# A hybrid transformer layer in one launch: the joints of its two MLP products, and which engine multiplies in its closing norm

## The chip, the cores and the metric

The kernel runs on one core of a Trainium2 chip. The metric is the device time of one launch, in microseconds. The core's engines are called as in the profile: PE is TensorE (matmuls), PEld its weight load, DVE is VectorE, ACT ScalarE, POOL GpSimd, and SP (SyncE) issues the DMAs of the queue that matters here. Each engine works through its own list of instructions in order; semaphores make one wait for another.

## What is computed

One layer on 2048 tokens of width 1024, in fp32: a modulated input projection feeds attention heads and RWKV heads, an output projection joins them, and a norm and an MLP close the layer. The change concerns the last two lines of this, the end of the first norm and the whole MLP (hidden width 4096):

```python
def layer_norm(x, gain, bias):
    return (_normalize(x, LN_EPS) * gain + bias).astype(x.dtype)
def squared_relu_mlp(h, w1, w2):
    return jnp.square(jax.nn.relu(h @ w1)) @ w2
...
x = layer_norm(ALPHA * x + g1 * y, ln1_g, ln1_b)
x = layer_norm(ALPHA * x + g2 * squared_relu_mlp(modulate(x, sh2, sc2), mlp_w1, mlp_w2), ln2_g, ln2_b)
```

## The kernel before

A scheduler (the tile framework) takes the instructions in program order and sets from it, from the buffers and from the data each needs, the order in which each engine gets them. Loads and stores of these stages stand in SyncE's queue in the order in which they are issued. A named tile has a number of buffers (bufs); a new use of it waits until the oldest user is done.

**Seven products.** Both MLP products are done as 2x2 blocks by a scheme with seven block products in place of eight. The products are worked in the order MORD = (1, 5, 6, 3, 7, 2, 4). Operands are sums and differences of blocks. Each operand is held as two parts: a high part, cast to the format that TensorE takes (fp32r) by ScalarE, and a low part, the operand less its high part, made by VectorE. Each block pair then takes three matmuls: high by high, high by low, low by high.

**First product, mlp1.** The weights come in 32 groups, 16 for each half of the tokens; a group is one 128x8x256 tile (1.05 MB) in one of two buffers. Per group seven products of 12 matmuls each (L1513). prep(n) makes the weight operand of product n, three products ahead of the matmuls (M1LEAD): a sum on VectorE where there is one (w1s, L1438 to L1447), the cast w1h on ScalarE (L1452), the low part w1l on VectorE (L1453). When product 4 of group g is prepared, its buffer is done with, and the weights of group g+2 are loaded. The token operands are made once for each half: those of products 1, 5 and 6 before mlp1 starts (xstep), and those of 3, 7, 2 and 4 are written to DRAM (XU), read back by xload, and split by xsplit into xh (ScalarE, L1465) and xl (VectorE, L1466). The norm of the last two token tiles (xlast, norm1, L1351 to L1360) is done within groups 0 and 1; in it GpSimd multiplies by the gain (L1355), and VectorE adds the bias (L1356). Groups 4 to 11 also make the token operands for the second half. Results go through ReLU and square, are combined, and are stored to DRAM (HU, L1525).

**Second product, mlp2.** For each token half, four groups of hidden rows, each with seven products of one or two units. A unit is 24 matmuls (L1699) and takes a pair of hidden rows' tiles (al, 128x2x512, 0.52 MB, loaded from HU by hload, L1605) and weights (wp, 1.05 MB, wload, L1600). ScalarE casts ah and uh (L1654, L1610), VectorE makes the low parts (L1655, L1610). Ahead of the first hidden tile stand the four weight loads of the first group and two of the next. PSUM results are copied or added into acc (L1706, L1708).

**Closing, mlp_end.** At the end of each half what is left of the hidden rows (two of the sixteen blocks) is done as plain products (192 matmuls, L1782), with operands from std_prep (L1739). Eight rows of 128x1024 are finished one after the other: multiply by g2 (L1765, on VectorE for the rows in VMUL, otherwise on GpSimd), add ALPHA times the residual (L1766, VectorE), add the plain products from PSUM (L1784, VectorE, frees the buffers psqa and psqb), mean and variance (ScalarE, with small VectorE steps, L1795, L1799, L1800), multiply by the gain l2g (L1803, VectorE from row LGV on, otherwise GpSimd), add the bias l2b (L1804, VectorE), store. The last two rows of the second half are normalized on VectorE alone (L1787 to L1790). While half 0 is closed, the operands of half 1 are already being made.

## Time and profile before

| | us |
|---|---|
| three runs | 3502.34, 3503.34, 3514.05 |
| median | 3503.34 |
| profiled execution | 3507.75 |
| its span | 3506.0 |

The granted clock of TensorE, over the profiled span, is 0.954 of full speed. The first product's matmuls begin at 2180 us of the span, the second's at 2851.8, its second token half at about 3169, and the last matmul ends at 3485.5. The change touches nothing ahead of the output projection, whose end is at about 2160. Times in a timeline count from the span's start. "Idle before" is how long the engine stood still ahead of an instruction, and the name behind the arrow is what came last before it could start.

### The profile page before, as it was taken

The numbers are of one execution on the slowest core, as the hardware profiler recorded it, in microseconds if no ns is written. First come the engines' busy times: TensorE is split into PE (matmuls) and PEld (weight loads), VectorE is DVE, ScalarE is ACT, GpSimd is POOL, SyncE is SP. The second block draws the span as 40 slices with busy tenths as digits, with TensorE's granted clock in tenths as the row PEclk, the third lists the DMA queues.
The fourth block names the chain that finished last, engine by engine and source line by source line (L and its number), as shares of the span: only waits on it lengthen the run. The fifth ranks groups of instructions, "written<-read, shape, count | busy, mean of one in ns | idle before, by whom it ended". The sixth has DMA issues, their size and how long they took to land. (4 is left out here: it accounts for less than half of the span.)

```text
span 3506.0 us, 65269 instructions
## 1 busy us (share of the span) xinstructions
PE 3204.8 (91%) x25176; PEld 2608.2 (74%) x25176; DVE 2606.6 (74%) x4891; ACT 1522.6 (43%) x2891; POOL 553.2 (16%) x551
## 2 busy tenths in 40 slices
PE   7999999899948988899979987999999979999997
PEld 3878898789746766677756765777788858887886
DVE  5568887979696668668568867766767657898888
ACT  4555565456524444444532223333433344336433
POOL 0000000000013454444433321000000000021004
PEclk9999999999978999999989988999999989999998
DMA  7487367636775464554354546566544455445441
GB/s 247 134 245 216 86 175 183 174 97 171 196 181 136 99 147 115 131 124 124 94 175 152 165 149 216 192 196 210 206 156 141 147 178 169 160 160 193 146 156 66
DMA packets 765338, 561.67 MB, mean 160 GB/s; under 512 B 380412, under 2 KB 653564, under 8 KB 763620
## 3 DMA queue, kind: packets, MB, share of 16 engines
q1 hardware_dynamic: 691738, 523.14, 51.0%
q10 hardware_dynamic: 73290, 34.37, 3.4%
q8 instruction: 198, 3.24, 0.4%
q14 instruction: 112, 0.92, 0.1%
HBM read 359.70 MB, written 197.66 MB: 159 GB/s over the span
## 5 line engine op out<-in xcount | busy, mean ns | idle before, releaser
L449 PE MATMUL psm<-xh,wh 128*128 128x386 f32 (+1 forms) x1104 | 380.5, 347 | 16.0 <-ACT row L452 10.2
L449 PE MATMUL psm<-xl,wh 128*128 128x386 f32 (+1 forms) x1104 | 380.8, 345 | 2.4 <-DVE xl L420 2.2
L449 PE MATMUL psm<-xh,wl 128*128 128x386 f32 (+1 forms) x1104 | 377.0, 341 | 0.0
L449 PEld LDWEIGHTS psm<-xh,wh 128*128 128x128 f32 x1104 | 210.2, 191 | 42.2 <-ACT row L452 19.3
L1513 PE MATMUL psa<-xh,w1h 128*128 128x512 f32 x512 | 203.8, 398 | 25.9 <-ACT w1h L1452 19.7
L1765 POOL TENSOR_TENSOR acc<-acc,g 128x1024 f32<-128x1024 f32 x12 | 42.2, 3541 | 1154.6 <-DVE acc L1708 1154.6
L449 PEld LDWEIGHTS psm<-xl,wh 128*128 128x128 f32 x1104 | 210.4, 191 | 17.4 <-issue 7.3
L449 PEld LDWEIGHTS psm<-xh,wl 128*128 128x128 f32 x1104 | 210.3, 190 | 5.0 <-issue 3.7
L1654 ACT CAST ah<-al 128x1024 fp32r<-128x1024 f32 x98 | 103.0, 1051 | 235.2 <-DMA al<-HU 226.0
L1513 PE MATMUL psa<-xl,w1h 128*128 128x512 f32 x512 | 202.1, 395 | 0.0
L1513 PE MATMUL psa<-xh,w1l 128*128 128x512 f32 x512 | 201.0, 393 | 0.3 <-DVE w1l L1453 0.3
L1655 DVE TENSOR_TENSOR al<-al,ah 128x1024 fp32r<-128x1024 f32 x98 | 120.7, 1231 | 100.1 <-ACT ah L1654 99.9
L1699 PE MATMUL psqa<-uh,ah 128*128 128x512 f32 x400 | 156.9, 395 | 29.3 <-ACT uh L1610 22.2
L759 DVE TENSOR_TENSOR stmp<-mp,xp 128x9 f32<-128x9 f32 (+30 forms) x310 | 167.4, 540 | 20.9 <-DMA mp<-LB 8.9
L435 DVE TENSOR_TENSOR wl<-wst,wh 128x1024 fp32r<-128x1024 f32 x81 | 98.8, 1219 | 93.4 <-ACT wh L434 74.1
L1452 ACT CAST w1h<-w1s 128x512 fp32r<-128x512 f32 x96 | 59.6, 621 | 232.1 <-DVE w1s L1441 84.9
L1133 PE MATMUL psg<-ks,bkc 64*64 64x128 f32 (+1 forms) x1152 | 98.4, 289 | 65.2 <-DMA ks<-AR 63.1
L1699 PE MATMUL psqa<-ul,ah 128*128 128x512 f32 x400 | 156.9, 392 | 0.0
L1699 PE MATMUL psqa<-uh,al 128*128 128x512 f32 x400 | 156.6, 392 | 0.0
L760 DVE TENSOR_REDUCE xp<-stmp 128x3 f32<-128x9 f32 (+30 forms) x310 | 153.9, 497 | 3.4
L1699 PE MATMUL psqb<-ul,ah 128*128 128x512 f32 x384 | 149.4, 389 | 0.0
L1699 PE MATMUL psqb<-uh,al 128*128 128x512 f32 x384 | 149.4, 389 | 0.0
(394 smaller groups left out, 8932.3 us busy)
## 6 DMA issues: line engine op xcount, KB each, us to landing
al<-HU SPq DMA_DIRECT2D x106, 512.0 KB, 3.7
wst<-in_w_in SPq DMA_DIRECT2D x81, 512.0 KB, 4.5
w<-in_mlp_w SPq DMA_DIRECT2D x32, 1024.0 KB, 7.9
wp<-in_mlp_w SPq DMA_DIRECT2D x32, 1024.0 KB, 6.1
wmod<-in_w_mod SPq DMA_DIRECT2D x48, 512.0 KB, 5.1
HU<-p SPq DMA_DIRECT2D x96, 256.0 KB, 4.4
HU<-s SPq DMA_DIRECT2D x84, 256.0 KB, 2.0
bkc<-BK SPq DMA_DIRECT2D x36, 512.0 KB, 3.7
```

Source lines behind the costliest of these rows:

```text
L435: nc.vector.tensor_tensor(wl, w, f32(wh), ALU.subtract)
L449: nc.tensor.matmul(ps[:, :y - x], lhsT=s[:, k, :], rhs=m[:, k, x:y], start=(i == 0), stop=(i == 23))
L759: nc.vector.tensor_tensor(tv, mp[:, i:i + 1, lo:lo + n].to_broadcast([128, n, n]), xp[:, lo:lo + n, lo:lo + n], ALU.mult)
L760: nc.vector.tensor_reduce(xp[:, lo:lo + n, i], tv, AX.X, ALU.add)
L1133: nc.tensor.matmul(ps[u, p, 0:w], lhsT=bk[o, d, p, u], rhs=ks[h][o, d, p, 0:w], start=True, stop=True)
L1452: nc.scalar.copy(h, x)
L1513: nc.tensor.matmul(ps, lhsT=w[:, k, :], rhs=x[:, k, :], start=(i == 0 and pr in (1, 5, 2)), stop=(i == 11), skip_group_check=True)
L1654: fs += [lambda: nc.scalar.copy(ah, f32(al)), fb[0], lambda: V.tensor_tensor(al, f32(al), f32(ah), ALU.subtract), fb[1]]
L1655: lambda: V.tensor_tensor(al, f32(al), f32(ah), ALU.subtract), fb[1]]
L1699: nc.tensor.matmul(ps, lhsT=x[:, c, s], rhs=y[:, c, :], start=(i == 0 and new), stop=(i == 5 and end), skip_group_check=True)
L1765: (V if 4 * i + j in VMUL else G).tensor_tensor(row, row, g2, ALU.mult)
```

## The change

1. VMUL grows from rows (0, 1) to (0, 1, 2, 3) and LGV is removed. So GpSimd does eight of the g2 multiplies in place of twelve, and none of the twelve gain multiplies; VectorE does them.
2. The first two groups of mlp1 are interleaved: products 1, 5, 6 of both groups, then 3, 7, 2, 4 of both. The splits of loaded token operands come one product later and are issued behind the weight operand of a named product (issue_after, as elsewhere in this kernel). w1s gets four buffers.
3. The norm of the last two token tiles moves from groups 0 and 1 to 2 and 3, with its gain and bias rows loaded at group 1; the transposes move to groups 5 to 12.
4. At group 20 of mlp1 the first weights of mlp2 and the two hidden tiles of its first two units are loaded, into buffers that are free by then (m2first). The rows l2g, l2b and g2 get buffers of their own and are loaded at unit 8. The hidden tiles rotate over four buffers of one pool and two of another, in place of six of one. HU and XU become two DRAM tensors each, one for each half.
5. The loop that overlaps the output projection with the first xsteps does two of them per tile.

```diff
--- before.py
+++ after.py
@@ -49,8 +49,7 @@
 
-LGV = (6, 6)
-VMUL = (0,1)
+VMUL = (0, 1, 2, 3)
 CLEAD = 2
 
 
@@ -93,8 +92,8 @@
-        self.HU = scr("HU", [2, 16, 128, 7, 512])
-        self.XU = scr("XU", [2, 128, 7, 4, 512])
+        self.HU = [scr("HU%d" % i, [16, 128, 7, 512]) for i in range(2)]
+        self.XU = [scr("XU%d" % i, [128, 7, 4, 512]) for i in range(2)]
@@ -875,12 +874,14 @@
                     self.xu[pr] = [self.xp.tile([128, 4, 512], F32R, name="x%s%d" % (v, pr)) for v in "hl"]
                 self.w1 = {}
                 self.w1load(0)
-                m = 0
-                for i, _ in enumerate(tiles):
-                    for m in range(m, min(m + 3, 8)):
+                todo = list(range(8))
+                more = True
+                while more:
+                    for m in todo[:2]:
                         self.xstep(0, m // 2, m % 2)
-                    m += m < 8
-                assert m == 8
+                    del todo[:2]
+                    more = next(tiles, 0) is None
+                assert not todo
         with ExitStack() as e1:
             self.mlp1(e1)
         ex.close()
...
@@ -1424,8 +1425,10 @@
-        seq = [(g, pr) for g in range(NG) for pr in MORD]
-        sums, units = {}, {}
+
+        seq = [(g, pr) for ps in (MORD[:3], MORD[3:]) for g in range(2) for pr in ps]
+        seq += [(g, pr) for g in range(2, NG) for pr in MORD]
+        sums, units, made = {}, {}, {}
 
         def prep(n):
             if n >= len(seq):
@@ -1434,7 +1437,7 @@
             if pr == 5:
-                x = sums[g] = sp.tile([128, 4, 128], F32, name="w1s", bufs=2)
+                x = sums[g] = sp.tile([128, 4, 128], F32, name="w1s", bufs=4)
                 V.tensor_tensor(x, a21, a22, ALU.add)
             elif pr == 6:
                 x = sums[g]
@@ -1449,21 +1452,22 @@
                 x = {1: a11, 2: a12, 4: a22}[pr]
             h = up.tile([128, 4, 128], F32R, tag="w1u", name="w1h", bufs=10)
             l = up.tile([128, 4, 128], F32R, tag="w1u", name="w1l", bufs=10)
-            nc.scalar.copy(h, x)
-            V.tensor_tensor(l, x, f32(h), ALU.subtract)
+            made[n] = nc.scalar.copy(h, x).ins, V.tensor_tensor(l, x, f32(h), ALU.subtract).ins
             units[n] = h, l
...
         def xload(q, pr):
-            nc.sync.dma_start(f32(self.xu[pr][1]), self.XU[q, :, XU[pr]])
-
-        def xsplit(pr, src=None):
+            nc.sync.dma_start(f32(self.xu[pr][1]), self.XU[q][:, XU[pr]])
+
+        def xsplit(pr, n, src=None):
             h, l = self.xu[pr]
             src = f32(l) if src is None else src
-            nc.scalar.copy(h, src)
-            V.tensor_tensor(l, src, f32(h), ALU.subtract)
+            with self.tc.issue_after(made[n][0]):
+                nc.scalar.copy(h, src)
+            with self.tc.issue_after(made[n][1]):
+                V.tensor_tensor(l, src, f32(h), ALU.subtract)
 
...
-        todo = {n + 1: [lambda pr=pr: xsplit(pr)] for n, pr in enumerate(MORD[3:])}
+
+        todo = {n + 2: [lambda pr=pr, n=n: xsplit(pr, n + 3)] for n, pr in enumerate(MORD[3:])}
...
             if pr == 1:
-                if g < 2:
-
-                    if g == 0:
-                        rows = self.base.tile([128, 2, 1024], F32, tag="uk", name="l1gb")
-                        for i, v in enumerate(("ln1_g", "ln1_b")):
-                            nc.sync.dma_start(rows[:, i], a[v].to_broadcast([128, D]))
+                if g == 1:
+                    rows = self.base.tile([128, 2, 1024], F32, tag="uk", name="l1gb")
+                    for i, v in enumerate(("ln1_g", "ln1_b")):
+                        nc.sync.dma_start(rows[:, i], a[v].to_broadcast([128, D]))
+                elif g in (2, 3):
+
                     self.flush()
                     x, xn = [self.base.tile([128, 1024], F32, tag="t4", name=v, bufs=2) for v in ("xlast", "xnlast")]
-                    r = OB[-1] + g * 128
+                    r = OB[-1] + (g - 2) * 128
                     nc.sync.dma_start(x, self.X1[r:r + 128, :])
                     self.norm1(x, slice(r, r + 128), xn, rows[:, 0], rows[:, 1], osm)
-                elif g == 2:
+                elif g == 4:
                     self.flush()
-                elif 4 <= g < 12:
-                    if g == 4:
+                elif 5 <= g < 13:
+                    if g == 5:
                         self.uk = self.base.tile([128, 8, 256], F32, tag="uk", name="uk")
-                    self.xstep(1, (g - 4) // 2, g % 2)
+                    self.xstep(1, (g - 5) // 2, (g - 5) % 2)
                 elif g == 14:
                     u1 = self.base.tile([128, 4, 512], F32, tag="uk", name="u1")
-                    nc.sync.dma_start(u1, self.XU[1, :, XU[1]])
+                    nc.sync.dma_start(u1, self.XU[1][:, XU[1]])
+                elif g == 20:
+
+                    w = self.base.tile([128, 2, 1024], F32, tag="uk", name="wp")
+                    nc.sync.dma_start(w, self.w2rows(0, 0))
+                    hs = [self.hload(self.base, "t4", 2, 0, 2 * i, 1) for i in range(2)]
+                    self.m2first = w, hs
...
-                    xsplit(1, u1)
+                    xsplit(1, n + 1, u1)
                 else:
                     xload(1, pr)
-                    todo.setdefault(n + 4, []).append(lambda pr=pr: xsplit(pr))
+                    todo.setdefault(n + 4, []).append(lambda pr=pr, n=n: xsplit(pr, n + 5))
...
+    def w2rows(self, fg, i):
+        return self.a["mlp_w2"].rearrange("(c i p) n -> i p c n", i=2, p=128)[i, :, fg:fg + 2, :]
+
+    def hload(self, pool, tag, bufs, half, fg, pr):
+        t = pool.tile([128, 2, 512], F32R, tag=tag, name="al", bufs=bufs)
+        self.nc.sync.dma_start(f32(t), self.HU[half][fg:fg + 2, :, XU[pr]].rearrange("c p t -> p c t"))
+        return t
 
 
 
@@ -1581,9 +1601,8 @@
-        nc.sync.dma_start(g2, self.G[1].to_broadcast([128, D]))
-        lg, lb = [self.base.tile([128, D], F32, tag="t4", name=x, bufs=2) for x in ("l2g", "l2b")]
-        cnt = [0]
+        lg, lb = [cp.tile([128, D], F32, name=x) for x in ("l2g", "l2b")]
+        cnt = [1, 2]
 
         def c8(name):
             cnt[0] += 1
@@ -1594,16 +1613,15 @@
         def u3(name):
             return up.tile([128, 2, 512], F32R, tag="u3", name=name, bufs=16)
 
-
         def wload(fg, i):
             t = c8("wp")
-            nc.sync.dma_start(t, a["mlp_w2"].rearrange("(c i p) n -> i p c n", i=2, p=128)[i, :, fg:fg + 2, :])
+            nc.sync.dma_start(t, self.w2rows(fg, i))
             return t
 
         def hload(half, fg, pr):
-            t = up.tile([128, 2, 512], F32R, tag="al", name="al", bufs=6)
-            nc.sync.dma_start(f32(t), self.HU[half, fg:fg + 2, :, XU[pr]].rearrange("c p t -> p c t"))
-            return t
+            cnt[1] += 1
+            pool, tag, bufs = (self.base, "t4", 2) if cnt[1] % 6 in (1, 2) else (up, "al", 4)
+            return self.hload(pool, tag, bufs, half, fg, pr)
 
         def split(x):
             h, l = u3("uh"), u3("ul")
@@ -1663,18 +1681,23 @@
                 f()
             del fs[:k]
 
-        for f in wloads(0, 0):
+        ws[0, 0, 0, 0], (hs[0], hs[1]) = self.m2first
+        first = wloads(0, 0)[1:]
+        for n in range(2, M2LEAD + ALEAD):
+            if first:
+                first.pop(0)()
+            aload(n, 0)
+        for f in first:
             f()
-        for n in range(M2LEAD + ALEAD):
-            aload(n, 0)
         for n in range(M2LEAD):
             for f in lead(n):
                 f()
-        for t, x in ((lg, "ln2_g"), (lb, "ln2_b")):
-            nc.sync.dma_start(t, a[x].to_broadcast([128, D]))
         for n, (half, g, pr, kk) in enumerate(seq):
             m = n + M2LEAD
             aload(m + ALEAD, half)
+            if n == 8:
+                for t, x in ((lg, a["ln2_g"]), (lb, a["ln2_b"]), (g2, self.G[1])):
+                    nc.sync.dma_start(t, x.to_broadcast([128, D]))
...
-                (V if r >= LGV[half] else G).tensor_tensor(row, row, lg, ALU.mult)
+                V.tensor_tensor(row, row, lg, ALU.mult)
                 V.tensor_tensor(row, row, lb, ALU.add)
             t = base[4 * i + j]
             nc.sync.dma_start(a["out"][t:t + 128, :], row)
```

ScalarE's list at the entry of mlp1, before; xh<-xl is the split of a loaded token operand, w1h the cast of a weight operand (w a loaded block, w1s a sum):

```order
L1385 CAST xh_24328<-uk 128x256
L1465 CAST xh_25079<-xl_25080 128x2048
L1452 CAST w1h<-w_24330 128x512
L1452 CAST w1h<-w1s 128x512
L1465 CAST xh_25081<-xl_25082 128x2048
L208 ACTIVATE ors<-omv,eps 128x1
L1452 CAST w1h<-w1s 128x512
L1465 CAST xh_25083<-xl_25084 128x2048
```

The same place after the change:

```order
L1386 CAST xh_24330<-uk 128x256
L1455 CAST w1h<-w_24332 128x512
L1455 CAST w1h<-w1s 128x512
L207 ACTIVATE ors<-omv,eps 128x1
L1455 CAST w1h<-w1s 128x512
L1455 CAST w1h<-w_25111 128x512
L1468 CAST xh_25081<-xl_25082 128x2048
L1455 CAST w1h<-w1s 128x512
```

The first weight casts stood behind a token operand's cast, and that one behind its load; now four weight casts stand ahead of it.

SyncE's queue between the products, before; HU<-p and HU<-z are the last stores of mlp1, g the row g2:

```order
L1525 DMA HU<-p_30089 128x512
L1584 DMA g_30199<-G_93 128x1024
L1600 DMA wp<-in_mlp_w 128x2x1024 x2
L1525 DMA HU<-z_30171 128x512
L1600 DMA wp<-in_mlp_w 128x2x1024 x4
L1605 DMA al<-HU 128x2x512 x12
L1600 DMA wp<-in_mlp_w 128x2x1024
```

The same place after the change (HU_90 and HU_91 are the two halves' tensors):

```order
L1536 DMA HU_91<-p_30097 128x512
L1618 DMA wp<-in_mlp_w 128x2x1024 x3
L1536 DMA HU_91<-z_30179 128x512
L1618 DMA wp<-in_mlp_w 128x2x1024 x3
L1700 DMA l2g<-in_ln_g 128x1024
L1700 DMA l2b<-in_ln_b 128x1024
L1700 DMA g_30207<-G_95 128x1024
L1590 DMA al<-HU_90 128x2x512 x10
L1618 DMA wp<-in_mlp_w 128x2x1024
```

The first load of hidden rows in this place stood behind one row and six weight loads; it is now the third unit's, and stands behind six weight loads and three rows.

VectorE's list between the halves, before; acc<-psqa and acc<-psqb are the additions that free the PSUM buffers:

```order
L1784 TENSOR_TENSOR acc<-psqa,acc 128x512
L1795 TENSOR_SCALAR zmu<-zmu 128x1
L1804 TENSOR_TENSOR acc<-acc,l2b 128x1024
L1799 RECIPROCAL zrs_32314<-zrs_32314 128x1
L1800 TENSOR_SCALAR znb<-zmu,zrs_32314 128x1
L1784 TENSOR_TENSOR acc<-psqb,acc 128x512
L1804 TENSOR_TENSOR acc<-acc,l2b 128x1024
L1799 RECIPROCAL zrs_32375<-zrs_32375 128x1
L1795 TENSOR_SCALAR zmu<-zmu 128x1
L1784 TENSOR_TENSOR acc<-psqa,acc 128x512
```

The same place after the change:

```order
L1807 TENSOR_TENSOR acc<-psqa,acc 128x512
L1827 TENSOR_TENSOR acc<-acc,l2b 128x1024
L1823 TENSOR_SCALAR znb<-zmu,zrs_32272 128x1
L1826 TENSOR_TENSOR acc<-acc,l2g 128x1024
L1818 TENSOR_SCALAR zmu<-zmu 128x1
L1822 RECIPROCAL zrs_32316<-zrs_32316 128x1
L1807 TENSOR_TENSOR acc<-psqb,acc 128x512
L1827 TENSOR_TENSOR acc<-acc,l2b 128x1024
L1823 TENSOR_SCALAR znb<-zmu,zrs_32316 128x1
L1826 TENSOR_TENSOR acc<-acc,l2g 128x1024
L1807 TENSOR_TENSOR acc<-psqa,acc 128x512
```

Between one psqa addition and the next stood two bias additions; now two bias additions and two gain multiplies stand there.

## Rows read from the trace of the kernel before

**Rows 1.** Busy table of the page: engine, busy us, share of the span, instructions.
```profile
PE 3204.8 (91%) x25176; PEld 2608.2 (74%) x25176; DVE 2606.6 (74%) x4891; ACT 1522.6 (43%) x2891; POOL 553.2 (16%) x551
```

**Rows 2.** TensorE's timeline, entry: start, us, instruction, partitions x elements, [idle before <-releaser].
```profile
2180.02 0.79 PE L1513 MATMUL psa<-xh,w1h 128*128 128x512 f32 x1 [19.38 <-ACT w1h L1452]
```

**Rows 3.** ScalarE's timeline, entry of the first product.
```profile
2177.55 1.90 ACT L1465 CAST xh<-xl 128x2048 fp32r<-128x2048 f32 x1 [12.96 <-DMA xl<-XU]
```

**Rows 4.** VectorE's timeline, entry of the first product.
```profile
2174.34 0.69 DVE L1438 TENSOR_TENSOR w1s<-w 128x512 f32<-128x512 f32 x1 [6.17 <-DMA w<-in_mlp_w]
...
2195.24 1.22 DVE L1356 TENSOR_TENSOR xlast<-xlast,l1gb 128x1024 f32<-128x1024 f32 x1 [2.27 <-POOL xlast L1355]
```

**Rows 5.** Windows: stretch, us, engines' busy time; then one of L1513 alone (PE, PEld).
```profile
2174.30:2236.50 62.20, 50.93 (x199) 38.74 (x200) 53.66 (x79) 26.16 (x41) 8.41 (x2) 0.90 0.59 217
...
2228.45:2248.75 20.30, 19.39 (x85) 15.57 (x84) 1.00 0.72 232
```

**Rows 6.** GpSimd's timeline, entry of the first product.
```profile
2189.18 6.02 POOL L1355 TENSOR_TENSOR xlast<-xlast,l1gb 128x1024 f32<-128x1024 f32 x1 [38.36 <-DMA l1gb<-in_ln_b]
```

**Rows 7.** ScalarE's timeline, between the products.
```profile
2830.29 0.63 ACT L1560 ACTIVATE z<-z 128x512 f32<-128x512 f32 x1
...
2849.79 1.04 ACT L1654 CAST ah<-al 128x1024 fp32r<-128x1024 f32 x1 [18.87 <-DMA al<-HU]
```

**Rows 8.** TensorE's timeline, between the products.
```profile
2851.83 2.07 PE L1699 MATMUL psqa<-uh,ah 128*128 128x512 f32 x4 [22.21 <-ACT uh L1610]
```

**Rows 9.** Windows of L1699 alone: us, PE, PEld, granted clock, DMA share, GB/s.
```profile
2835.00:2850.00 15.00, 0.00 (x0) 0.00 (x0) 0.50 1.02 410
2851.80:2864.90 13.10, 13.07 (x48) 10.64 (x49) 0.83 0.41 149
2864.90:2875.80 10.90, 10.90 (x49) 9.01 (x48) 1.00 0.34 98
```

**Rows 10.** TensorE's timeline, between the halves.
```profile
3169.78 0.50 PE L1699 MATMUL psqa<-uh,ah 128*128 128x512 f32 x1 [1.27 <-DVE zmu L1795]
...
3177.30 0.80 PE L1699 MATMUL psqa<-uh,ah 128*128 128x512 f32 x1 [5.87 <-DVE acc L1784]
```

**Rows 11.** Window of all engines after the second of these waits.
```profile
3177.30:3186.00 8.70, 8.70 (x32) 7.07 (x33) 8.70 (x8) 7.84 (x11) 3.89 (x1) 0.81 0.87 301
```

**Rows 12.** VectorE's timeline, between the halves.
```profile
3160.10 0.68 DVE L1784 TENSOR_TENSOR acc<-psqa,acc 128x512 f32<-128x512 f32 x1
...
3169.71 1.21 DVE L1804 TENSOR_TENSOR acc<-acc,l2b 128x1024 f32<-128x1024 f32 x1
3170.84 0.15 DVE L1799 RECIPROCAL zrs<-zrs 128x1 f32<-128x1 f32 x1
...
3173.17 3.36 DVE L1804 TENSOR_TENSOR acc<-acc,l2b 128x1024 f32<-128x1024 f32 x1 [1.34 <-POOL acc L1803]
...
3176.57 0.68 DVE L1784 TENSOR_TENSOR acc<-psqa,acc 128x512 f32<-128x512 f32 x1
```

**Rows 13.** Window of the closing stretch, all engines (DVE is the third).
```profile
3435.00:3503.00 68.00, 50.43 (x222) 41.08 (x220) 57.14 (x73) 24.64 (x40) 37.49 (x12) 0.89 0.13 54
```

**Rows 14.** VectorE's timeline, closing; the last row is its last instruction.
```profile
3480.51 3.40 DVE L1804 TENSOR_TENSOR acc<-acc,l2b 128x1024 f32<-128x1024 f32 x1 [1.38 <-POOL acc L1803]
...
3501.06 1.28 DVE L1790 SCALAR_TENSOR_TENSOR acc<-acc,zrs,l2b 128x1024 f32<-128x1024 f32 x1
```

**Rows 15.** GpSimd's timeline, closing (two instructions).
```profile
3477.29 5.53 POOL L1803 TENSOR_TENSOR acc<-acc,l2g 128x1024 f32<-128x1024 f32 x2 [0.35 <-ACT acc L1801]
```

**Rows 16.** VectorE's groups, 3110 to 3506: xcount | busy, mean ns | idle before, releaser.
```profile
L1766 DVE SCALAR_TENSOR_TENSOR acc<-x,acc 128x1024 f32<-128x1024 f32 x16 | 29.5, 1850 | 0.0
...
L1804 DVE TENSOR_TENSOR acc<-acc,l2b 128x1024 f32<-128x1024 f32 x14 | 23.5, 1681 | 7.7 <-POOL acc L1803 7.7
...
L1739 DVE TENSOR_TENSOR al<-al,uh 128x1024 fp32r<-128x1024 f32 x6 | 14.9, 2485 | 2.7 <-ACT uh L1739 2.7
```

More of the change, by code (lines that the diff above doesn't have):

```diff
@@ L1402, in xstep @@
         i = 3 if q == 0 else 0
-        nc.sync.dma_start(self.XU[q, :, i:7, k, cs], self.uk[:, i:7])
+        nc.sync.dma_start(self.XU[q][:, i:7, k, cs], self.uk[:, i:7])
     def w1load(self, g):
@@ L1505, in mlp1 @@
             if pr in (1, 5, 2):
-                st[bank] = psP.tile([128, 512], F32, name="ps" + bank, bufs=2)
-            ps = st[bank]
+                st[bank, g] = psP.tile([128, 512], F32, name="ps" + bank, bufs=2)
+            ps = st[bank, g]
             h, l = units.pop(n)
@@ L1537, in mlp1 @@
             elif pr == 7:
-                z12, z22 = st["p", 6], st["p", 5]
+                z12, z22 = st["p", 6, g], st["p", 5, g]
                 V.tensor_tensor(z22, ps, z22, ALU.add)
@@ L1542, in mlp1 @@
                 if not std:
-                    s = st["s1"] = T("s1")
+                    s = st["s1", g] = T("s1")
                     V.tensor_tensor(s, z12, z22, ALU.add)
@@ L1546, in mlp1 @@
             elif pr == 2:
-                z12, z11 = st["p", 6], st["p", 1]
+                z12, z11 = st["p", 6, g], st["p", 1, g]
                 V.tensor_tensor(z11, ps, z11, ALU.add)
@@ L1551, in mlp1 @@
                 if not std:
-                    s = st["s2"] = T("s2")
-                    V.tensor_tensor(s, st["s1"], z11, ALU.subtract)
+                    s = st["s2", g] = T("s2")
+                    V.tensor_tensor(s, st["s1", g], z11, ALU.subtract)
                     V.tensor_tensor(z12, z11, z12, ALU.subtract)
@@ L1562, in mlp1 @@
                 if not std:
-                    s4, s2 = T("s4"), st["s2"]
+                    s4, s2 = T("s4"), st["s2", g]
                     def last(q=q, fg=fg, z21=z21, s4=s4, s2=s2):
                         V.tensor_tensor(s4, z21, s2, ALU.subtract)
-                        nc.sync.dma_start(self.HU[q, fg, :, XU[3]], s4)
+                        nc.sync.dma_start(self.HU[q][fg, :, XU[3]], s4)
                     todo.setdefault(n + 1, []).append(last)
```

6 lines of the change are left out of this document (3 added, 3 removed).

## The prediction

> **What bounds the kernel now.** I read the page's busy table first: TensorE is busy for 91% of the span, VectorE 74% [rows 1]. So the time is TensorE's own work plus the places where it stands still, and only those can change here, since the matmuls stay the same in number and size. Then TensorE's timeline, for what ended each idle stretch. Four joints remain. At the entry into the first MLP product it idles 19.38 us [rows 2]. Between the MLP products it idles 22.21 us [rows 8]. Between the two token halves of the second product it idles 1.27 and 5.87 us [rows 10]. After its last matmul, at 3485.5, VectorE goes on to 3502.34 [rows 14]. Last I read the timelines of VectorE, ScalarE and GpSimd in those four stretches, since the joints differ in what ends last.
>
> The profiled execution took 3507.75 us (span 3506.0 and 1.75 around it), 4.4 above the median 3503.34. I make the sum against 3507.75 and take the 4.4 off at the end.
>
> **Entry of the first product.** Before, ScalarE's queue has the cast of a loaded operand (xh<-xl) ahead of the first weight cast; it waits for the load until 2177.55 [rows 3], and the first matmul starts at 2180.02 [rows 2]. The change puts the weight casts first and lets the first six products (1, 5, 6 of two groups) use operands that are already in SBUF. From 2180.0 to 2236.5 TensorE ran 199 matmuls, which at the third group's pace (85 in 20.30) would take 47.5 of the 56.5 us [rows 5]; so TensorE alone could win about 9 us here, some of it clock, and the early start covers what it waits for. But VectorE makes the low parts of all operands, and in 2174.3 to 2236.5, which covers the work for three groups, it is busy 53.66 of 62.2 us [rows 5]. The change takes none of these instructions away, it only reorders them; the wait for the first weight load until 2174.34 [rows 4] stays too, as that load is where it was. So the end of this work can come at most 8.5 us sooner. Of the 8.5 the wait of 2.27 for GpSimd [rows 4] may go, and the one for the xh cast with it. New ones come: the third group's weights are asked for only when the first group's last operand is made, which now stands behind ten products' preparation rather than seven, and VectorE's next sum waits for that load. GpSimd's two norm multiplies now fall into a busy VectorE: the one at 2189.18 took 6.02 us because VectorE's splits held it off until they ended [rows 6], and once it runs it holds VectorE off. I keep 7 of the 8.5 us: TensorE then runs ahead in the first two groups and waits some 6 us in the third. Taken: 1.5 us gained. Ends: 8.5 (all idle goes), and 3 lost (that wait is followed by a stretch at the lower clock, as the one of 5.87 us below, and a weight load comes late).
>
> In the later groups the norm and the transposes move one group on, and issue the same loads as before. I cost them at nothing; VectorE is hidden behind a group's matmuls there, and if that cover fails it is 1 to 2 us, in either direction.
>
> **Between the products.** Before, the first tile of hidden rows is loaded behind g2 and six weight loads and lands at 2849.7 [rows 7]; the transfers run at 410 GB/s [rows 9], so this is a queue of bytes. After, the weights and the two hidden tiles of the first two products are loaded long before. ScalarE is free at 2830.92 (2830.29 plus 0.63 [rows 7]) and needs two casts of 1.04, so the first matmul can start at about 2833: 3.3 us of idle. Two products are 48 matmuls, 13.1 us after a restart (granted clock 0.83 over them, and 0.50, the lower level of 1.2 and 2.4 GHz, in the idle stretch before) [rows 9]; they end at about 2846. The third product's hidden tile stands behind six weight loads of 1.05 MB, a 0.26 MB store and three row broadcasts of 0.52 MB, with itself 8.65 MB, 21 us at 410 GB/s: landed at about 2852, cast by 2854. TensorE idles 8 us more. So the 49th matmul starts at 2854 instead of 2864.9: 10.7 us gained, of which a second restart at the lower clock takes back 2.2 (13.1 against 10.9 for 48 [rows 9]). Taken: 8. Ends: 10.7 (no second slow restart), and 3, if the tile comes 5 us later because the row broadcasts move slower than the other bytes, which no row of before shows.
>
> **Between the halves.** TensorE waits for VectorE's additions, which free the psqa buffers: at 3169.78 and 3177.30 [rows 10]. VectorE is late because of GpSimd. Its bias addition takes 1.21 us alone, but 3.36 when GpSimd's next multiply runs, and it first waits 1.34 us for GpSimd's result [rows 12]. From the psqa addition at 3160.10 to that at 3176.57 are 16.47 us [rows 12]. After, seven multiplies and bias additions stand between the same two (4 gains, 3 biases) at 1.13 (3169.71 to 3170.84, the start of the next instruction [rows 12]), four psq additions at 0.6 (0.68 less the same overlap) and eight small ones at 0.15: 11.5 us. That is 5 us sooner, so 2.1 of TensorE's 5.87 + 1.27 us remain. Ahead of it, two more g2 multiplies cost VectorE 2.4 us and two collisions fewer give back about 3 (below). The lower clock after 3177.30 cost 1.5 us (32 matmuls in 8.70 us at a granted clock of 0.81 [rows 11], instead of 7.25 at the pace of 48 in 10.9); whether 2.1 us of idle lead there is open, and I count the 1.5 as gained. Gain 5 + 1.5 + 0.6 (the 3 less the 2.4), about 7. Ends: 8.6 (both waits and the clock), and 0.
>
> **Closing.** From 3435.0 to 3502.3, 67.3 us, VectorE is busy 57.1 [rows 13, 14]. The GpSimd multiplies by g2 lengthen VectorE's scaled additions and splits: (1.85 - 1.21) x 16 and (2.49 - 1.21) x 6, 17.9 us for twelve, 1.5 each; the multiplies by l2g its bias additions: (1.68 - 1.21) x 14, 0.55 each [rows 16]. Without six of each, VectorE's work is 57.1 - 9.0 - 3.3 = 44.8. It gains 8 multiplies at 1.21, 9.7; four g2 multiplies stay on GpSimd, 6.0: 60.5. Of its 10.2 us idle, half of 7.7 was for GpSimd [rows 16] and goes; of the 6.3 for ScalarE a fuller VectorE keeps perhaps 3. So 63.5 against 67.3: 3.8, taken as 3.5. Ends: 6.8 gained, 2.4 lost (collisions of 2.2 each, all waits for ScalarE). GpSimd's own end then matters to nobody.
>
> The collision, first by the rows: the bias addition at 3480.51 takes 3.40 instead of 1.21 and ends 1.09 after GpSimd's second multiply, which ends at 3482.82 [rows 14, 15]. The Trainium skill (SBUF — State Buffer, Who interferes with whom) states that a VectorE instruction with two SBUF inputs and a GpSimd one that reads SBUF exclude each other for the whole instruction. By it the four that stay cost up to 2.2 us each, 8.8 rather than 6.0, and the closing gains 0.7.
>
> **Sum.** 1.5 + 8 + 7 + 3.5 = 20; 3507.75 - 20 = 3487.75; less 4.4, 3483. By 0.5%, 17.5 us, a measurement can tell this kernel from no change: the border is 3485.8.
>
> **Rivals.**
> *VectorE follows at the entry* (0.15): all 8.5 us go, 7 more: 3476. For it, 8.5 us of idle in the stretch; against it, the weight loads.
> *The third hidden tile is late* (0.15): 3 instead of 8 between the products: 3488. For it, a queue already at 410 GB/s, with 1 MB more ahead of that tile than stood ahead of the first one before.
> *VectorE keeps half of the norm's gain* (0.15): 5.3 instead of 10.5 between the halves and in the closing: 3489. For it, VectorE is busy 57 of 67 us there already.
> *VectorE becomes the bound* (0.05), slower: the sixteen multiplies moved (8 per half) are paid in full at 1.21, 19.4 us, in the last rows of each half, and the collisions saved are eaten by waits for ScalarE, so that both norm terms turn: 3503.3 - 1.5 - 8 + 19.4 = 3513. It decides once VectorE's psqa addition comes later, counted from the start of the second half, than the one at 3176.57 did. For it, the busy share; against it, 17.9 + 6.6 us of that busy time are collisions and 7.7 us idle are GpSimd's [rows 16], over the two halves.
> The Trainium skill (Perfetto Trace Analysis, Optimizing Scalar/DVE Operations) speaks for this last rival: where VectorE is saturated, work may be better off on ScalarE or even GpSimd, the opposite of this change; it adds that between those two it might not help, as they share a port. The row of 3.40 us is on the side of that second half.
>
> **Chances.** The forecast 0.50, on its own 3474 to 3491. Faster by over 0.5%: two thirds of 0.50, all of the first rival, a quarter of the next two: 0.56. Slower: 0.04. Within 0.5%: 0.40. The range, 3470 to 3498, leaves out the slow rival and the sum of all best ends.
>
> **What would show it.** Entry: the first matmul near 2165, the second weight cast well before 2177, then a wait of TensorE of several us in the third group for an operand cast; without that wait the first rival holds. Between the products: two idle stretches, about 3 and 8 to 10 us, the second ended by the load of a hidden tile. Between the halves: no idle over 2.5 us, bias additions of 1.2 us, four GpSimd multiplies a half. Closing: VectorE almost without idle to the end, 13 to 14 us after the last matmul instead of 16.9. The prediction is wrong if a long idle appears in the middle of either product (the hidden tiles now have four buffers in one ring and two in another), or the second half starts later than it did.

## The result, and the profile after

The changed kernel takes 3479.47 us (median of 4, 3474.77 to 3481.47) against 3504.46 (median of 4): a ratio of 0.9921, 95% interval 0.9900 to 0.9943, so 20 to 35 us faster. Forecast were 3483 and 20 us.

The two profiled executions differ by 33.0 us (3507.75 and 3474.77). Of these 12.8 lie ahead of the change: the output projection's last matmul ends at 2160.64 before and at 2147.81 after, though up to there the order of instructions is the same on every engine (but for a few matmuls that start within 0.1 us of each other). In the fourteen profiles of this study that point lies between 2147.8 and 2172.0. So I count every stage from it; each column is one execution. The table is worked out from the starts and ends of the matmuls in each trace (us; "after" is the changed kernel, the other columns are experiments below):

| stage | before | after | norm_back | g2_back | entry_back | joint_back | norm_only |
|---|---|---|---|---|---|---|---|
| A: output projection to the fourth group | 88.3 | 86.3 | 86.7 | 85.8 | 88.3 | 85.7 | 88.6 |
| B: to the first product's end | 580.7 | 579.0 | 579.7 | 581.3 | 583.8 | 580.5 | 582.2 |
| C: to the 97th matmul of the second | 46.2 | 39.5 | 39.4 | 39.8 | 39.3 | 45.6 | 46.0 |
| D: to the end of the first half's groups | 245.0 | 246.6 | 246.6 | 246.6 | 246.6 | 245.0 | 245.0 |
| E: to the 49th matmul of the second half | 65.0 | 55.8 | 66.5 | 62.7 | 56.0 | 55.7 | 55.6 |
| F: to the end of its groups | 255.8 | 257.5 | 257.5 | 257.5 | 257.5 | 255.8 | 255.8 |
| G: its plain products | 43.9 | 44.0 | 44.3 | 44.2 | 44.0 | 43.5 | 43.5 |
| H: to the span's end | 20.5 | 16.4 | 21.8 | 19.3 | 16.0 | 16.9 | 16.6 |
| all | 1345.4 | 1325.1 | 1342.4 | 1337.2 | 1331.5 | 1328.8 | 1333.3 |

From the output projection on, the change gains 20.3 us: 2.0 in A, 1.6 in B, 6.7 in C, 9.2 in E, 4.0 in G and H, less 1.6 in D and 1.6 in F. How far single executions scatter shows in the kernels of this study that are alike in a stage. Among the seven with the changed kernel's entry (after, norm_back, g2_back, joint_back, queue_short, al_pool, g2_all) A goes from 85.4 to 88.5 and B from 578.0 to 581.3. In the same way C goes from 39.2 to 39.8 in the seven kernels with its loads between the products, E from 55.6 to 56.0 and H from 16.0 to 17.6 in the seven with its closing; D and F agree within 0.1. So the 1.6 in B is not told from scatter, nor is the 2.0 in A by itself (see entry_back).

TensorE's timeline after, at the same joints as [rows 2, 8, 10]:

```profile
2152.56 0.79 PE L1524 MATMUL psa<-xh,w1h 128*128 128x512 f32 x1 [4.75 <-ACT w1h L1455]
...
2166.72 0.80 PE L1524 MATMUL psb<-xh,w1h 128*128 128x512 f32 x1 [12.95 <-ACT w1h L1455]
...
2217.83 0.79 PE L1524 MATMUL pse<-xh,w1h 128*128 128x512 f32 x1 [4.75 <-ACT w1h L1455]
...
2816.36 0.50 PE L1722 MATMUL psqa<-uh,ah 128*128 128x512 f32 x1 [3.23 <-ACT uh L1628]
...
2839.21 0.80 PE L1722 MATMUL psqb<-uh,ah 128*128 128x512 f32 x1 [9.77 <-ACT uh L1628]
...
3147.96 0.50 PE L1722 MATMUL psqa<-uh,ah 128*128 128x512 f32 x1 [0.93 <-DVE acc L1807]
```

The 19.38 us at the entry have become 4.75 and, two matmuls later, 12.95, with a new wait of 4.75 in the third group. The 22.21 us between the products have become 3.23 and 9.77. Between the halves 0.93 is left of 1.27 and 5.87.

ScalarE's timeline after, the casts that end two of these waits [rows 3, 7]:

```profile
2166.05 0.62 ACT L1455 CAST w1h<-w1s 128x512 fp32r<-128x512 f32 x1 [13.55 <-DMA X<-xres]
...
2837.17 1.04 ACT L1672 CAST ah<-al 128x1024 fp32r<-128x1024 f32 x1 [8.26 <-DMA al<-HU]
```

The first waits for a store that the prediction did not name: the weight operand lies where the output projection's result lay, and that must have left for DRAM. The second is the third unit's hidden tile.

VectorE's timeline after, at the places of [rows 4, 12, 14], and its groups from 3080 to the end, as [rows 16]:

```profile
2161.73 0.69 DVE L1441 TENSOR_TENSOR w1s<-w 128x512 f32<-128x512 f32 x1 [6.25 <-DMA w<-in_mlp_w]
...
3148.95 1.22 DVE L1827 TENSOR_TENSOR acc<-acc,l2b 128x1024 f32<-128x1024 f32 x1
...
3467.76 1.28 DVE L1813 SCALAR_TENSOR_TENSOR acc<-acc,zrs,l2b 128x1024 f32<-128x1024 f32 x1
```

```profile
L1789 DVE SCALAR_TENSOR_TENSOR acc<-x,acc 128x1024 f32<-128x1024 f32 x16 | 25.7, 1613 | 0.0
L1826 DVE TENSOR_TENSOR acc<-acc,l2g 128x1024 f32<-128x1024 f32 x14 | 17.1, 1219 | 2.2 <-ACT acc L1824 2.2
L1827 DVE TENSOR_TENSOR acc<-acc,l2b 128x1024 f32<-128x1024 f32 x14 | 17.0, 1217 | 0.0
...
L1762 DVE TENSOR_TENSOR al<-al,uh 128x1024 fp32r<-128x1024 f32 x7 | 8.5, 1221 | 5.4 <-ACT uh L1762 5.4
```

The bias additions' mean fell from 1681 to 1217 ns and their 7.7 us of waiting for GpSimd are gone. The splits went from 2485 to 1221. The gain multiplies cost 17.1 us that VectorE did not have before, and still the tail after the last matmul is 12.6 us (3456.48 to 3469.04), not 16.9. The windows after the two restarts of the second product, as [rows 9] (L1722 alone):

```profile
2816.36:2829.40 13.04, 13.04 (x48) 9.84 (x48) 0.87 0.99 393
2839.21:2852.60 13.39, 13.39 (x48) 10.88 (x49) 0.81 0.42 147
```

Both restarts run below the full clock; the second is new, and costs 13.39 instead of 10.90.

### The profile page after: what moved, and what is told of

It reads as the page before. It is cut to its first block, busy times and chain, and to the rows that moved or that the text cites. A ratio compares the mean times of both kernels' runs of the same rounds, so it can differ in the third digit from the quotient of the medians.

```text
span 3472.9 us, 65271 instructions
## 1 busy us (share of the span) xinstructions
PE 3196.9 (92%) x25176; PEld 2602.5 (75%) x25176; DVE 2610.7 (75%) x4907; ACT 1523.3 (44%) x2891; POOL 507.8 (15%) x535
## 4 chain that ended last, share of the span: by engine, by line
PE 66%; DVE 15%; DMA 10%; issue 3%; ACT 3%; SPq 3%; ACTq 0%; POOL 0%; DVEq 0%; POOLq 0%
PE psm L448 13%; PE psa L1524 10%; PE psqb L1722 7%; PE psqa L1722 7%; PE psb L1524 5%; PE ops L1339 3%; PE pse L1524 2%; DMA ks<-AR 2%; PE psv L1044 2%; PE psm L466 2%; PE psg L1134 1%; DVE stmp L758 1%; PE pst L1015 1%; PE psl L979 1%; DMA qz<-Q 1%
## 5 line engine op out<-in xcount | busy, mean ns | idle before, releaser
L448 PE MATMUL psm<-xh,wh 128*128 128x386 f32 (+1 forms) x1104 | 381.0, 347 | 15.5 <-ACT row L451 10.3
L448 PEld LDWEIGHTS psm<-xl,wh 128*128 128x128 f32 x1104 | 210.6, 191 | 17.6 <-DVE xl L419 7.6
L1788 POOL TENSOR_TENSOR acc<-acc,g 128x1024 f32<-128x1024 f32 x8 | 28.9, 3639 | 1188.4 <-DVE acc L1731 1188.4
L1673 DVE TENSOR_TENSOR al<-al,ah 128x1024 fp32r<-128x1024 f32 x98 | 121.4, 1239 | 88.4 <-ACT ah L1672 88.3
L1722 PE MATMUL psqa<-uh,ah 128*128 128x512 f32 x400 | 155.0, 391 | 4.2 <-ACT uh L1628 3.2
L1722 PE MATMUL psqb<-uh,ah 128*128 128x512 f32 x384 | 149.8, 393 | 9.8 <-ACT uh L1628 9.8
L1722 PE MATMUL psqa<-ul,ah 128*128 128x512 f32 x400 | 157.3, 393 | 0.0
L1722 PE MATMUL psqa<-uh,al 128*128 128x512 f32 x400 | 156.8, 392 | 0.0
L1722 PE MATMUL psqb<-ul,ah 128*128 128x512 f32 x384 | 151.0, 393 | 0.0
```

The source lines that it names most:

```text
L448: nc.tensor.matmul(ps[:, :y - x], lhsT=s[:, k, :], rhs=m[:, k, x:y], start=(i == 0), stop=(i == 23))
L1673: lambda: V.tensor_tensor(al, f32(al), f32(ah), ALU.subtract), fb[1]]
L1722: nc.tensor.matmul(ps, lhsT=x[:, c, s], rhs=y[:, c, :], start=(i == 0 and new), stop=(i == 5 and end), skip_group_check=True)
```

## The experiments

Each is the changed kernel with one edit, except norm_only (the kernel before with one). Ratios are to the kernel before, run on the same chip. Where a part is worth a few us, the stages above decide, since the intervals of the ratios are 9 to 17 us wide: by the ratios alone only norm_back and best_pad can be told from the changed kernel (0.9900 to 0.9943).

**norm_back: the closing undone.**

```diff
-VMUL = (0, 1, 2, 3)
+LGV = (6, 6)
+VMUL = (0, 1)
-                V.tensor_tensor(row, row, lg, ALU.mult)
+                (V if r >= LGV[half] else G).tensor_tensor(row, row, lg, ALU.mult)
```

> The changed kernel with the closing alone undone: twelve g2 multiplies and the twelve gain multiplies are GpSimd's again. If the prediction's account of collisions is right, the wait between the halves returns (some 7 us of idle on TensorE, bias additions of 3.4 us), and the closing grows from 13 to about 17 us after the last matmul: together 11 us slower than the changed kernel (7 + 4), the rest of it unmoved. Rival (VectorE is the bound there, and the earlier second half came from the loads): the second half starts as early as in the changed kernel and the time moves by less than 3 us.

Ratio 0.9973 (0.9960 to 0.9986). Stage E is back at 66.5 and H at 21.8: 17.3 us lost in all, of which E takes 10.7 and G and H 5.6. That is more than the 7 and 4 that were expected, and more than the 13.2 that the change gained in these stages. TensorE, VectorE, and the window after the wait (engines as in [rows 11]):

```profile
3175.31 0.80 PE L1723 MATMUL psqa<-uh,ah 128*128 128x512 f32 x1 [5.88 <-DVE acc L1808]
```

```profile
3163.59 3.40 DVE L1828 TENSOR_TENSOR acc<-acc,l2b 128x1024 f32<-128x1024 f32 x1 [1.05 <-POOL acc L1827]
...
3171.16 3.37 DVE L1828 TENSOR_TENSOR acc<-acc,l2b 128x1024 f32<-128x1024 f32 x1 [1.33 <-POOL acc L1827]
```

```profile
3175.30:3184.80 9.50, 9.49 (x31) 7.54 (x32) 9.50 (x10) 8.43 (x12) 3.89 (x1) 0.72 0.79 277
```

The wait, the long additions and the lower clock come back together, as in [rows 10 to 12]. The rival falls.

**norm_only: the closing's change alone, in the kernel before.** The same edit the other way round.

> The kernel before with the closing's change alone (eight g2 and twelve gain multiplies to VectorE's side as in the change; nothing else). If the closing's gain is its own and does not need the other parts: the stretch from the first half's last matmul of four groups to the 48th of the second half goes from 65.0 to 56 us, the tail after the last matmul from 20.5 to 16.5: 13 us faster than the kernel before, a ratio of 0.9963. If it needs the rows' own buffers or the new order of loads, less than 8 us.

Ratio 0.9954 (0.9930 to 0.9978). E 55.6, H 16.6, G 43.5: 13.7 us by these three, against 13 expected and 13.2 in the changed kernel. VectorE's bias additions in it:

```profile
L1803 DVE TENSOR_TENSOR acc<-acc,l2b 128x1024 f32<-128x1024 f32 x14 | 17.0, 1212 | 0.0
```

So this part stands by itself, and is two thirds of the gain.

**g2_back: only the four g2 multiplies back on GpSimd** (VMUL = (0, 1)).

> Only the four g2 multiplies that moved (two in each half) go back to GpSimd; the gains stay on VectorE. By the prediction's prices VectorE saves 4 x 1.21 = 4.8 us and pays 4 collisions of 1.5 (6.0): +1 us; by collisions of 2.2 (8.8): +4 us, spread over both halves. If VectorE's own work is the bound and collisions are hidden: 2 to 5 us faster.

Ratio 0.9940 (0.9924 to 0.9957). E is 6.9 longer than after, H 2.9: 9.8 us with G, more than either price. VectorE has six lengthened instructions there in a half, beside six GpSimd multiplies (10.9 us above 1.21 each), against four (7.0): 3.9 more, less 2.4 for the multiplies that it is rid of. The rest is TensorE's, by its timeline and the window behind the second wait:

```profile
3119.34 0.50 PE L1805 MATMUL psqb<-uh 128*128 128x512 f32 x1 [1.28 <-DVE acc L1731]
...
3163.18 0.80 PE L1722 MATMUL psqa<-uh,ah 128*128 128x512 f32 x1 [3.52 <-DVE acc L1807]
```

```profile
3163.20:3172.50 9.30, 9.30 (x28) 7.45 (x29) 9.30 (x10) 8.35 (x13) 0.00 (x0) 0.68 0.70 226
```

The changed kernel behind its wait of 0.93:

```profile
3148.00:3155.00 7.00, 7.00 (x30) 5.70 (x31) 7.00 (x9) 7.00 (x13) 0.00 (x0) 1.00 0.90 308
```

Waits of 3.52 and 1.28 instead of 0.93 are 3.9 us. After them 28 matmuls take 9.30 us at a granted clock of 0.68; at the changed kernel's pace (30 in 7.00) 6.5: 2.8 more. These two make 6.7 of the 6.9. Idle of 0.93 us cost no clock, idle of 3.52 did.

**g2_all: all g2 multiplies on VectorE** (VMUL = tuple(range(8))).

> The changed kernel with the last eight g2 multiplies on VectorE too, so none on GpSimd in the closing. By the prediction's collisions (1.5 to 2.2 us each, against 1.21 for the multiply) VectorE's work falls by 2 to 8 us over both halves, and the time by as much or less. By what going back by four multiplies cost (9.8 us by the stages of that run), more: up to 15. If VectorE is saturated by then, slower by up to 9.7.

Ratio 0.9940 (0.9921 to 0.9960). E 54.6, H 15.7: 2.1 us better than after by these two, outside the scatter of both, the low end of what was expected. No instruction of VectorE is lengthened any more and TensorE waits nowhere over 0.6 us between the halves; there is no more clock to win back.

**entry_back: the first two groups in the old order.**

```diff
-        seq = [(g, pr) for ps in (MORD[:3], MORD[3:]) for g in range(2) for pr in ps]
-        seq += [(g, pr) for g in range(2, NG) for pr in MORD]
+        seq = [(g, pr) for g in range(NG) for pr in MORD]
...
-        todo = {n + 2: [lambda pr=pr, n=n: xsplit(pr, n + 3)] for n, pr in enumerate(MORD[3:])}
+        todo = {n + 1: [lambda pr=pr: xsplit(pr)] for n, pr in enumerate(MORD[3:])}
```

> The changed kernel with the order of the first two groups' products and splits as before (the norm of the last tiles stays in groups 2 and 3). If the new order is what gains at the entry, the stretch from the last matmul of the output projection to the end of the first product is 3.7 us longer than in the changed kernel. If the gain is due to the norm's move out of groups 0 and 1 (the wait of 2.27 us and GpSimd's 6 us multiply), it is unchanged, within 1 us.

Ratio 0.9936 (0.9917 to 0.9954). TensorE's first matmul:

```profile
2183.73 0.79 PE L1527 MATMUL psa<-xh,w1h 128*128 128x512 f32 x1 [19.31 <-ACT w1h L1454]
```

A is 88.3 as before, 2.0 more than after. B is 4.8 more, 2.5 of it up to the second half's start; the rest lies where nothing was changed, and g2_back has 1.9 of the like there. A alone does not decide, since queue_short has the new order and 88.5 too. A and B together do: they take 669.0 to 672.1 us in the three kernels with the old order (before, norm_only, entry_back) and 664.3 to 667.1 in the seven with the new, 4.8 less on the mean. For this run against the changed kernel it is 6.8; expected were 3.7. So the order gains, between 2 and 8 us. The norm's move gains nothing that can be seen: of the three, the one in which it has moved, entry_back, is the slowest.

**joint_back: the loads between the products as before.** The block at g == 20 and m2first are taken out, hload uses six buffers of one pool, the rows are loaded where they were.

> The changed kernel with the loads between the products as before (nothing loaded ahead, six buffers in one pool, rows as before). One idle stretch of about 22 us in place of 3.2 and 9.8 us, no second restart at the lower clock: 48 matmuls later the stage is 5.7 us longer than in the changed kernel, and the rest is the same. If the gain there were the run's own scatter, less than 3 us.

Ratio 0.9950 (0.9934 to 0.9967).

```profile
2850.61 0.80 PE L1710 MATMUL psqa<-uh,ah 128*128 128x512 f32 x1 [22.02 <-ACT uh L1621]
```

C is 45.6, 6.1 more than after (5.7 expected). But D and F are each 1.6 shorter, at 245.0 and 255.8 as before the change. So this part is worth 6.1 less 3.2.

**queue_short: less in the queue ahead of the third hidden tile.**

```diff
-        self.nc.sync.dma_start(f32(t), self.HU[half]...)
+        self.hdma.append(self.nc.sync.dma_start(f32(t), self.HU[half]...).ins)
...
+                        if half == g == 0:
+                            with self.tc.issue_after(self.hdma[3]):
+                                f()
...
+                with self.tc.issue_after(self.hdma[3]):
+                    for t, x in ((lg, ...), (lb, ...), (g2, ...)):
```

> The changed kernel, but between the products the next group's three weight loads and the three row broadcasts are issued behind the third and fourth unit's hidden tiles. If the second idle stretch (9.8 us in the changed kernel) is a queue of bytes, 4.7 MB less ahead of that tile at 410 GB/s is 11.5 us: the tile lands before the first two units are through, the idle stretch is gone and with it the second restart at the lower clock (13.4 instead of 10.9 us for 48 matmuls): 12 us faster than the changed kernel up to the 96th matmul. Rival (the tile waits for its buffer's memory or for a fixed latency, not for the bytes ahead of it): the idle stretch keeps more than 5 us.

Ratio 0.9933 (0.9916 to 0.9950). ScalarE and TensorE:

```profile
2846.12 1.04 ACT L1677 CAST ah<-al 128x1024 fp32r<-128x1024 f32 x1 [6.91 <-DMA al<-HU]
```

```profile
2848.16 0.79 PE L1728 MATMUL psqb<-uh,ah 128*128 128x512 f32 x1 [2.88 <-ACT uh L1629]
```

The tile is cast 12.9 us after the first product's end (2833.27), in the changed kernel 24.0: 11.2 sooner, against 11.5 from the bytes. The bytes' account holds. C is 32.1, 7.4 less than after and not 12, because in the new order TensorE's list has the third unit's first matmul after 28 of the first 48, and still meets it 2.9 us early.

**pool_swap: weight operands and hidden results change places in SBUF.**

```diff
-        self.srcp, sp, up, zp = P("w1src"), P("w1sum"), P("w1u"), P("h1")
+        self.srcp, sp, zp, up = P("w1src"), P("w1sum"), P("h1"), P("w1u")
```

> The changed kernel with the pools of weight operands and of hidden results in the other order in SBUF. In the changed kernel's trace the second weight cast (the second product's) waits 13.55 us for the store X<-xres, whose tile lay where the weight operands lie now. With the swap they lie over the output projection's operands, which are free at its last matmul. If that wait is what the entry ends on, TensorE's idle of 12.95 us goes and the fourth group starts some 9 us sooner. Rival (VectorE's list and the second group's weight load bind, as the prediction has it): only VectorE's idle of 2.5 us behind that cast goes, the fourth group starts 2 to 4 us sooner, and TensorE waits more in the third group. Between the products the loads also come in another order, as the hidden tiles' memory is free earlier: the second idle stretch shrinks there too, to be read apart.

Ratio 0.9910 (0.9893 to 0.9927). TensorE's waits at the entry and between the products, then VectorE at the second of them, then ScalarE's second weight cast:

```profile
2170.32 0.79 PE L1524 MATMUL psa<-xh,w1h 128*128 128x512 f32 x1 [6.87 <-ACT w1h L1455]
...
2180.09 0.79 PE L1524 MATMUL psa<-xh,w1l 128*128 128x512 f32 x1 [7.08 <-DVE w1l L1455]
...
2232.23 0.80 PE L1524 MATMUL pse<-xh,w1h 128*128 128x512 f32 x1 [5.22 <-ACT w1h L1455]
...
2831.15 1.45 PE L1722 MATMUL psqa<-uh,ah 128*128 128x512 f32 x4 [3.23 <-ACT uh L1628]
```

```profile
2177.55 0.69 DVE L1441 TENSOR_TENSOR w1s<-w 128x512 f32<-128x512 f32 x1 [6.52 <-DMA w<-in_mlp_w]
...
2179.36 0.67 DVE L1455 TENSOR_TENSOR w1l<-w,w1h 128x512 fp32r<-128x512 f32 x1
```

```profile
2171.12 0.62 ACT L1455 CAST w1h<-w1s 128x512 fp32r<-128x512 f32 x1 [0.85 <-DVE w1s L1441]
```

The store's wait is gone, and A is only 1.0 shorter (85.3), within its scatter and less than the 2 to 4 of the rival, let alone 9. VectorE waits for the second group's weights with the first product's low part queued behind that wait, and the third group waits 5.22 again. So the first account falls, and the rival's is borne out in kind, if not in size: in this order VectorE's list and the second group's load set the end of the entry. Between the products no second wait is left: C is 27.1, 12.4 less than after. There the third hidden tile stands in the queue behind one weight load of those six, and is cast 10.3 us after the first product's end, which agrees with the bytes' account.

**aligned: 32 bytes left free.**

```diff
+                self.pool(eb, "pad", 1, side="right").tile([128, 8], F32, name="pad")
                 self.base = self.pool(eb, "base", 1, side="right")
```

> The changed kernel with 32 bytes left free at the top of the right-hand pools, so that the tiles of the pools base and xp begin at multiples of 64 bytes in SBUF, and not 32 behind one. In the changed kernel's trace a triple of matmuls takes 0.694 us in mlp2's units whose hidden tile lies in base, and 0.680 in all others; in mlp1 a matmul takes 0.232 to 0.235 with the token operands of products 1, 5 and 6 (pool xp), 0.227 with the others. If the address does it, all go to 0.227: 1.6 us for each half of the second product and about 7 us of the first, 10 in all. If it is the products' place in the order or the other engines' traffic, nothing changes.

Ratio 0.9937 (0.9916 to 0.9957). D and F stay at 246.6 and 257.5: the guess on the address is wrong. Two units in this kernel, the first with its tile in base:

```profile
2870.13:2875.68 5.55, 5.55 (x25) 4.51 (x24) 1.00 0.68 200
2881.23:2886.67 5.44, 5.44 (x25) 4.51 (x24) 1.00 0.80 275
```

A is 8.2 us shorter (78.1), which I did not expect; the ratio is too coarse to show it. The shift also changed the order of the transposes ahead of the entry; which of the two does it was not told apart. Stage A of the changed kernel and of this one, all engines (DVE is the third):

```profile
2147.81:2234.13 86.32, 63.88 (x253) 51.01 (x254) 67.56 (x102) 30.84 (x50) 6.74 (x2) 0.84 0.68 233
2161.76:2239.86 78.10, 61.91 (x252) 48.95 (x253) 60.96 (x92) 29.72 (x47) 8.64 (x2) 0.89 0.69 241
```

VectorE does ten instructions and 6.6 us less before the fourth group starts, five of them steps that combine results of earlier groups, which come later here. The second weight cast still waits 11.50 us for the store. So what stands ahead in VectorE's list counts, and that wait does not.

**al_pool: the hidden tiles in one pool.**

```diff
-            cnt[1] += 1
-            pool, tag, bufs = (self.base, "t4", 2) if cnt[1] % 6 in (1, 2) else (up, "al", 4)
-            return self.hload(pool, tag, bufs, half, fg, pr)
+            return self.hload(up, "al", 6, half, fg, pr)
```

> The changed kernel with all hidden tiles of the second product in six buffers of one pool, as before the change; only the two that are loaded ahead keep their place in base. In the kernels with the change's two rings the stretch from the 96th matmul to the half's end takes 246.56 us, in the one without 244.96, and a unit whose hidden tile lies in base takes 5.55 instead of 5.44. If the tile's place costs this, both halves lose 1.6 us: 3.2 us faster than the changed kernel, nothing else moved. If it is another part of the joint's change (the loads' order, the rows' place), the stretch stays at 246.56.

Ratio 0.9926 (0.9912 to 0.9941). D is 245.0 and F 255.8: 3.2 us, as expected. (H is 1.1 longer here, 17.6, the longest of its seven.) The same two units in the changed kernel and then here (windows of the second product's line; 24 matmuls each):

```profile
2863.48:2869.03 5.55, 5.55 (x25) 4.50 (x24) 1.00 0.71 210
2874.58:2880.02 5.44, 5.44 (x26) 4.50 (x24) 1.00 0.82 282
```

```profile
2871.97:2877.41 5.44, 5.44 (x25) 4.51 (x24) 1.00 0.66 181
2882.85:2888.29 5.44, 5.44 (x25) 4.51 (x24) 1.00 0.84 262
```

**best and best_pad: what helped, together** (pool_swap, al_pool, g2_all; the second with the 32 bytes).

> The changed kernel with the pools of weight operands and hidden results swapped, six buffers in one pool for the hidden tiles, and all g2 multiplies on VectorE. From the end of the output projection to the end of the span: 1311.6 us (the swap alone), less 3.2 for the tiles' place and 2 to 3 for the multiplies: 1305 to 1306, against 1325.1 for the changed kernel and 1345.4 before, if the parts add. A ratio to the kernel before of 0.9887.

> The same with the 32 bytes left free at the top of the right-hand pools. These left every matmul's pace as it was (246.56 us again), but with them the first product ended 7 us earlier after the output projection, in an order of the transposes that the shift brought about. If that belongs to the order and adds to the rest: 1299 us in the place of 1305. If it was one execution's luck in the arrival of loads, as best, within 2 us.

best: ratio 0.9884 (0.9866 to 0.9901), median 3470.14, 1308.3 us from the output projection on; the parts add up but for 2 us, by which B is longer than in pool_swap. best_pad: 0.9872 (0.9855 to 0.9889), median 3464.07, 1302.8 us. By stages 4.9 of the 5.5 us between them are in A (84.8 and 79.9), but the two intervals overlap, so the times don't tell them apart. By stages they are 16.8 and 22.3 us faster than the changed kernel; the interval of best still touches that of the changed kernel, the one of best_pad lies clear of it.

## Why the prediction was right

**Entry: near in size, with a bound that does not hold.** Taken were 1.5 us, measured 2.0 in A. The new order is worth more, 4.8 us on the mean over A and B (entry_back), so 1.5 was low and its nearness to 2.0 is in part luck. The first matmul came 4.75 us after the output projection, as forecast, and the third group waits 4.75 for an operand (forecast some 6). What I had not seen is the wait of 12.95 behind two matmuls, for a store out of memory that the weight operands reuse. With it one sign failed: the second weight cast was to come well before 2177, which is 16.4 us after the output projection, and came 18.2 after it. The wait cost next to nothing on its own (pool_swap): VectorE's list behind the second group's load sets the same end. The step that failed is the bound of 8.5 us. It took VectorE's work in this stretch as fixed, but some of it can stand behind the fourth group's start: in aligned A is 10.2 us shorter than before. The later groups, taken at nothing, gave 1.6, which is within B's scatter.

**Between the products: right at the joint, 3.2 us given back later.** Forecast: idle of 3.3 and 8 us, a restart that takes back 2.2, gain 8. Measured: 3.23 and 9.77, 2.5, gain 6.7. The third tile was cast 24.0 us after the first product's end; forecast was a landing after 22.4, of which 21 are bytes at 410 GB/s. Cutting the bytes ahead of it brought it forward by the bytes' share (queue_short). The step that failed is a term put at nothing: the hidden tiles' new buffers have none in the sum, and cost 3.2 us. Two of six tiles now lie in base, and the units that read them run 2% longer (al_pool). The prediction named the two rings, but only as a danger of a long idle; there is none, the matmuls themselves are slower.

**Between the halves: right in mechanism, too small.** Forecast 7 with a best end of 8.6, measured 9.2. Of these 7.4 are idle time of TensorE (1.19, 1.27 and 5.87 us before, 0.93 after), and the rest is its clock. The wait of 1.19, in the plain products of half 0, had no term in the sum:

```profile
3130.11 0.50 PE L1782 MATMUL psqb<-uh 128*128 128x512 f32 x1 [1.19 <-DVE acc L1708]
```

The sum left 2.1 us of idle and left open whether that costs clock; 0.93 was left and did not. The price of a collision was right (1.75 us on each of four instructions, forecast 1.5 to 2.2). That g2's two multiplies would be worth only 0.6 was wrong: alone they are worth 6.9 there (g2_back), since with them back on GpSimd TensorE idles 3.9 us more and then loses 2.8 to a lower clock.

**Closing: right.** 4.0 against 3.5; the tail after the last matmul 12.6 against 13 to 14.

The sum, 20 against 20.3 by stages, is nearer than its terms, and that is luck: the forecast was 2.2 too low at the halves, 2.1 at the entry and the later groups and 0.5 in the closing, and 4.5 too high between the products. The medians differ by 25.0 us, 5 more than forecast.

**The rivals.** *VectorE follows at the entry* fell for this order (2.0 of 8.5 us). *The third hidden tile is late* fell: the tile came less than 2 us later than forecast, and the joint gained 6.7, not 3. *VectorE keeps half of the norm's gain* and *VectorE becomes the bound* fell with norm_only and g2_all (13.2 us by E, G and H, not 5.3 and not a loss): VectorE does fill its time there, but even eight more multiplies are cheaper than the collisions. In each half six GpSimd multiplies by g2 lengthen six instructions of VectorE (g2_back), four lengthen four (the changed kernel), and with none left (g2_all) none is lengthened. The Trainium skill's rule that a VectorE instruction with two SBUF inputs contends with a GpSimd one that reads SBUF (SBUF — State Buffer, Who interferes with whom) agrees with these runs: all the lengthened ones have two such inputs.

## What to carry to other kernels

Price work on GpSimd by what it does to VectorE's instructions beside it, and add TensorE's clock: here a wait of 3.52 us cost 2.8 more behind it (g2_back), one of 0.93 nothing. When a wait at the head of a chain goes, look for what stands next in each engine's list, for memory that is reused, and for a load with other work queued behind it; here the wait for a loaded operand hid one for a store, and that one hid the load of the second group's weights. Count unchanged stages from a common point, for one execution's scatter (here 24 us ahead of the changed part) can exceed the gain.

## What the runs showed of the hardware that I had not expected

In these kernels a matmul's pace depends on where its operand lies in SBUF (al_pool changes only the pool of these tiles): 24 matmuls take 5.55 us with the hidden tile in the pool at the top of SBUF and 5.44 with it in the lower pool, at a granted clock of 1.00 in both; by the starts of the matmuls three in a row, one of which has that tile as its loaded operand, take 0.694 instead of 0.680 us. A shift by 32 bytes does not remove it. What it is about the place stays open.
